# Queries and half of the output gates with the merge gates, scores two chunks ahead, linear attention's heads turn by turn

## The chip, the cores and the metric

One Trainium2 chip, of which the kernel uses one core, with its engines TensorE (PE; its weight loads are PEld), VectorE (DVE), ScalarE (ACT), GpSimd (POOL) and SyncE (SP, which here issues DMAs). The metric is the device time of one execution in microseconds (us), lower is better. All data are float32.

## What is computed

One block of a hybrid model on 1024 frames and 16 meta tokens of width 1024: a feed-forward part, then a mixing part with two branches (attention in a window with sinks, and gated linear attention), then a second feed-forward part. Cut to the mixing part:

```python
u = rmsnorm(h, mix_norm)
(aq, ak, av, gq, gk, gv, gr, g_low, gate_a, gate_b) = split(u @ w_in)
ya = window_sink_attention(aq, ak, av, att_sinks)     # 8 heads of 64, 2 of keys, chunks of 64
log_a = log_sigmoid(g_low @ gla_gate_w + gla_gate_b) / 16
og = gated_linear_attention(gq, gk, gv, log_a)        # 4 heads: 64 of keys, 128 of values
yb = rmsnorm(og, gla_out_norm) * silu(gr)
mixed = sigmoid(gate_a) * (ya @ w_branch_att) + sigmoid(gate_b) * (yb @ w_branch_gla)
h = h + mixed @ w_out
```

The widths are 512 for `aq`, `gv` and `gr` each, 256 for `gq` and `gk`, 128 for `ak` and `av`, and 1024 for each merge gate. Linear attention keeps a state S of each head, S_t = diag(a_t) S_(t-1) + k_t v_t, with output q_t S_t, in chunks: a causal product of scaled queries and keys inside of a chunk, and the state that the chunks before left.

## The kernel before, in words

A float32 matrix is kept as two parts, a high one and the rest (`split`, L101 and L102; weights by `wt.cut`, L125 and L126), and a product of two such matrices is three matmuls: high by high, high by low, low by high (L96 to L98). Columns of `w_in` are taken in blocks of 128, frames in pieces of 512 columns (`CH_FR`) or, with the meta tokens, of 512, 256 and 272 (`CH_T`). So a block over all frames is 2 x 24 matmuls of 512 columns, 96 for two blocks.

Large products go in another way: `Group.product` (L454) makes the four quarters of a product out of seven products of quarters and of their sums. For a pair of blocks these are seven times twelve, 84 matmuls of 512 columns. The sums are made on DVE or POOL (L437), the parts of the weights' quarters on ACT and DVE (L228, L229).

The mixing part in its order:

- **Plain projections** (`together`, L920 on): gk, gq and the first block of gr, as three matmuls each; ACT copies what comes out, and the results go to DRAM (`ev_keep`). As the inputs' parts are made here on ACT and DVE (L808, L812), the first ones run while they come in.
- **Merge gates** (loop at L1104): eight pairs of blocks by seven products. `gate_weights` loads a pair two turns before its use, `gate_out` applies a sigmoid to the first half and writes to `gates` in DRAM. In the last four pairs, `decay` also makes linear attention's scaled queries and keys, and writes them to DRAM.
- **Attention**: keys, values and queries are projected (`firsts`, `q_units`), then 16 chunks are worked off in a loop (L1400). `scores` makes the scores on PE, adds the bias and takes the maxima (L1294) on DVE, the exponentials on ACT (L1299), and scales on DVE (L1300, L1302). `turn` transposes the probabilities and splits them, `attend` multiplies with the values (L1333) and splits the result into `qs`. Scores are made one chunk ahead. To each chunk belongs a slot of `slots`: projections of gv and gr, whose outputs of values are turned later by PE (`ev_tok`, through the list `late`), and then products with `w_branch_att` (`branch_units`, tile `br`), which need attention's result.
- **Linear attention** (class `Gla`, L1446 on): twelve tiles of 512 KB are loaded through SP's queue (L1426). The four heads are two pairs, called heads 0 and 1 in the names; each takes eight steps. A step has the scores of the next step (`products`: tile `at`, L1483, and a masked copy on DVE, L1484), the products with values (`go`, L1490) and with the state (L1493), squares on ACT (L1497) and copies on DVE (L1498), and the update of the state (`kv` on PE, L1502, `st` on DVE, L1504). Head 0 runs all its steps, then head 1; branch products and the output gates (`out_gate`: sigmoid, product, transposes `ot`, and a split) stand between the steps. `end` scales a head's outputs by their norm (L1509 to L1513).
- **Branch products of linear attention** (L1571), then `w_out` and the second feed-forward part.

Outside of `manual_schedule` sections a scheduler orders each engine's instructions by what it assumes of their durations; a tile's next owner waits until the readers of the one before are done. `ttile` gives tiles from pools of four to eight (`g`, `a`, `ga` and more share them), `atile` from a pool of 16, which holds the inputs' parts, then linear attention's tiles.

## Time and profile before

| | us |
|---|---|
| median of 3 runs | 2015.7 |
| lowest and highest | 2015.16, 2017.0 |
| the profiled execution's own time | 2014.66 |
| its span in the trace | 2013.0 |
| PE busy | 1985.8 (99%) |
| DVE busy | 1405.2 (70%) |
| ACT busy | 894.6 (44%) |
| POOL busy | 176.0 (9%) |
| bytes moved by DMA | 343.03 MB, 170 GB/s in the mean |

The span runs from the first to the last instruction; the execution's own time has some us around it. A busy share is the part of the span in which an engine had an instruction in hand. Matmuls overlap in the records: a matmul of 512 columns shows 0.39 us, but the next one starts 0.23 us later, and it is the starts that tell how fast PE goes. The granted clock of PE is 0.997 of full speed in the mean.

### The profile page before, as it was taken

What the parts mean: (1) busy time and instruction counts of PE and PEld (TensorE: products, weight loads), DVE (VectorE), ACT (ScalarE), POOL (GpSimd) and SP (SyncE); (2) the same over time, 40 slices, a digit from 0 to 9 for tenths busy, and PEclk for the clock granted to TensorE, in tenths of its full rate; (3) what the DMA queues carried; (4) which work ended last, traced back from release to release, by engine and by line L of the source; (5) the groups of instructions that cost most, each with busy time, mean ns of one, the idle gap of its engine ahead of it and who ended that gap; (6) DMA issues with size and microseconds to landing.
All of it is one profiled execution on the core that took longest, in us unless ns stands there. A gap on an engine that the chain in (4) does not pass through costs nothing. (4 is left out here: it accounts for less than half of the span.)

```text
span 2013.0 us, 31814 instructions
## 1 busy us (share of the span) xinstructions
PE 1985.8 (99%) x11964; PEld 1757.2 (87%) x11964; DVE 1405.2 (70%) x2449; ACT 894.6 (44%) x1754; POOL 176.0 (9%) x210
## 2 busy tenths in 40 slices
PE   8999999999999999999999999999999999999998
PEld 8999999999999988888888767888888888878887
DVE  6976776675778785466467567568767766757786
ACT  6544444443322254465366445345444544442225
POOL 1000000002323000004100000110000000022220
PEclk9999999999999999999999999999999999999999
DMA  6243443349975333355212646741534543599832
GB/s 215 83 148 127 164 165 127 127 160 375 345 292 196 95 127 108 108 180 174 58 48 69 221 149 213 226 141 53 196 127 134 188 139 126 191 376 353 300 108 84
DMA packets 284618, 343.03 MB, mean 170 GB/s; under 512 B 26406, under 2 KB 192032, under 8 KB 284464
## 3 DMA queue, kind: packets, MB, share of 16 engines
q1 hardware_dynamic: 265376, 274.82, 41.7%
q10 hardware_dynamic: 17296, 61.29, 8.0%
q0 software_dynamic: 1792, 4.89, 0.7%
q8 instruction: 94, 1.54, 0.3%
q14 instruction: 60, 0.49, 0.1%
HBM read 220.66 MB, written 120.27 MB: 169 GB/s over the span
## 5 line engine op out<-in xcount | busy, mean ns | idle before, releaser
L454 PE MATMUL pb<-tt,wop 128*128 128x260 f32 (+1 forms) x2280 | 394.0, 326 | 1.1 <-ACT g L314 1.1
L454 PEld LDWEIGHTS pb<-tt,wop 128*128 128x128 f32 x2280 | 339.0, 188 | 38.3 <-ACT g L314 1.3
L229 DVE TENSOR_TENSOR wop<-s,wop 128x512 fp32r<-128x512 f32 x268 | 190.3, 713 | 116.6 <-ACT wop L228 116.1
L228 ACT CAST wop<-s 128x512 fp32r<-128x512 f32 x268 | 166.0, 621 | 233.9 <-PE pb L454 97.1
L454 PE MATMUL pb<-tm,wop 128*128 128x260 f32 (+1 forms) x1440 | 235.6, 319 | 6.0 <-ACT h L396 4.0
L454 PEld LDWEIGHTS pb<-tm,wop 128*128 128x128 f32 x1440 | 207.8, 189 | 25.9 <-ACT h L396 4.7
L228 ACT CAST wop<-raw 128x512 fp32r<-128x512 f32 x201 | 124.5, 621 | 221.6 <-PE pb L454 106.2
L229 DVE TENSOR_TENSOR wop<-raw,wop 128x512 fp32r<-128x512 f32 x201 | 143.8, 717 | 30.0 <-ACT wop L228 29.9
L454 PE MATMUL pd<-tt,wop 128*128 128x260 f32 (+1 forms) x792 | 138.7, 328 | 0.0
L454 PEld LDWEIGHTS pd<-tt,wop 128*128 128x128 f32 x792 | 118.9, 188 | 13.4
L341 DVE SCALAR_TENSOR_TENSOR h<-pb,h 128x520 f32<-128x520 f32 (+1 forms) x136 | 93.6, 692 | 38.3 <-PE pb L454 36.3
L454 PE MATMUL pd<-tm,wop 128*128 128x260 f32 (+1 forms) x720 | 119.3, 320 | 0.0
L454 PE MATMUL pb<-tb,wop 128*128 128x260 f32 (+1 forms) x696 | 115.7, 319 | 0.7 <-DVE m L742 0.7
L454 PE MATMUL pd<-tb,wop 128*128 128x260 f32 (+1 forms) x696 | 115.5, 319 | 0.0
L454 PE MATMUL pa<-tb,wop 128*128 128x260 f32 (+1 forms) x696 | 115.5, 319 | 0.0
L454 PEld LDWEIGHTS pd<-tm,wop 128*128 128x128 f32 x720 | 104.9, 190 | 9.4
L454 PEld LDWEIGHTS pb<-tb,wop 128*128 128x128 f32 x696 | 100.8, 188 | 10.5 <-ACT vec L87 0.7
L454 PEld LDWEIGHTS pd<-tb,wop 128*128 128x128 f32 x696 | 100.9, 188 | 9.6
L454 PEld LDWEIGHTS pa<-tb,wop 128*128 128x128 f32 x696 | 100.7, 188 | 9.8
L437 DVE TENSOR_TENSOR s<-raw 128x512 f32<-128x512 f32 x92 | 63.3, 688 | 58.6 <-DMA raw<-in_ffn_w_up 53.3
L96 PE MATMUL pj<-uh,whi 128*128 128x512 f32 (+2 forms) x256 | 91.5, 358 | 0.0
L437 POOL TENSOR_TENSOR s<-raw 128x512 f32<-128x512 f32 x28 | 37.7, 1346 | 601.7 <-DMA tm<-f2mid 427.9
(418 smaller groups left out, 3889.2 us busy)
## 6 DMA issues: line engine op xcount, KB each, us to landing
tm<-f1mid ACTq DMA_DIRECT2D x56, 520.0 KB, 6.2
tm<-f2mid ACTq DMA_DIRECT2D x56, 512.0 KB, 5.8
raw<-in_ffn_w_gate SPq DMA_DIRECT2D x42, 512.0 KB, 3.9
raw<-in_ffn_w_up SPq DMA_DIRECT2D x42, 512.0 KB, 4.0
raw<-in_ffn_w_down SPq DMA_DIRECT2D x80, 256.0 KB, 5.7
f2mid<-kh SPq DMA_DIRECT2D x70, 256.0 KB, 2.7
f2mid<-kl SPq DMA_DIRECT2D x70, 256.0 KB, 2.6
f1mid<-kh SPq DMA_DIRECT2D x63, 260.0 KB, 2.7
```

Source lines behind the costliest of these rows:

```text
L96: nc.tensor.matmul(ps, wh[k], xh[k], start=(k == 0), stop=False)
L228: nc.scalar.copy(x[:, 0:n], src)
L229: nc.vector.tensor_sub(x[:, n:2 * n], src, x[:, 0:n].bitcast(F32))
L341: nc.vector.scalar_tensor_tensor(hm, ps, 0.5, hm, op0=ALU.mult, op1=ALU.add)
L437: (eng.tensor_add if add else eng.tensor_sub)(a[s], a[x], a[y])
L454: nc.tensor.matmul(ps, y, z[:, s0:s0 + sn], start=(first and k == 0 and at == 0), stop=(at == 2 and k == len(cols) - 1), skip_group_check= ...
```

## The change

- The two blocks of gq and the blocks 2 and 3 of gr go into the loop of the merge gates as two more pairs, ahead of the eight (`PAIRS`). For gq, `gate_out` scales by 0.125; for gr it makes the sigmoid on ACT and, one product later, the product on DVE, so that `silu(gr)` is stored, and `out_gate` leaves both out for these blocks.
- In the plain projections, gv's blocks 0 and 1 and the first 512 columns of block 2 take the places of gq and of gr's block 0. Their transposes run one call of `together` later.
- Queries 0 and 1 are projected for the first 512 frames ahead of attention, and for the others in its slots. The slots hold those, the rest of gv, gr's blocks 0 and 1, and then the eight branch products that need only the first half of attention's result, as 2, 2, 2, 1 and 1. The weights of the branch and of three other blocks are loaded and cut a second time.
- `scores` runs two chunks ahead, with three tiles `p` in place of two; the reciprocal and the scaling are split off as `finish`.
- The loads of linear attention's tiles are issued on POOL's queue, three in each of the slots 11 to 14.
- The two heads take turns step by step; the masked scores (`attb`), the state and `km` have tiles of each head's own. `end` goes by halves. The output gates of the first half stand at steps 5 to 7 and behind the loop, those of the second half behind the last branch products. The first two branch weights of linear attention are used for the first half of the frames before the second.

```diff
-    plain_views = [cols_view(w_in, c) for c in (C_GK, C_GK + P, C_GQ, C_GQ + P, C_GR)]
+    plain_views = [cols_view(w_in, c) for c in (C_GK, C_GK + P, C_GV, C_GV + P, C_GV + 2 * P)]
...
+    plain_evac = [ev_keep(gk_dram[0]), ev_keep(gk_dram[1]), ev_tok(0), ev_tok(1), ev_tok(2)]
...
+    PAIRS = [("q", 0), ("r", 2)] + [("g", m) for m in range(0, 16, 2)]
...
+    def gate_out(at, i, c, x):
+        what, m = PAIRS[at]
+        cols = slice(c * 512, (c + 1) * 512)
+        if what == "q":
+            nc.scalar.activation(x, x, AF.Copy, scale=0.125)
+            nc.sync.dma_start(out=gq_dram[i, :, cols], in_=x)
+        elif what == "r":
+            g = ttile("g")
+            nc.scalar.activation(g, x, AF.Sigmoid)
+
+            def rest():
+                nc.vector.tensor_mul(x, x, g)
+                nc.sync.dma_start(out=gr_dram[m + i, :, cols], in_=x)
+            late.append(rest)
...
-    for m in range(0, 16, 2):
-        others = [decay(*x) for x in pieces.pop(0)] if m >= KT else []
+    for m in range(len(PAIRS)):
+        others = [decay(*x) for x in pieces.pop(0)] if len(PAIRS) - m <= 4 else []
...
-        s.p = ap_.tile([P, 4, W], F32, tag="p", name="p", bufs=2)
+        s.p = ap_.tile([P, 4, W], F32, tag="p", name="p", bufs=3)
...
+    slots = [[u] for u in (q_late[0], v_late[0], q_late[1], v_late[1], v_late[2], v_late[3], r_late[0], v_late[4], *r_late[1:])]
...
+    slots += [[fill.pop(0) for _ in range(n)] for n in (2, 2, 2, 1, 1)]
...
+        nc.gpsimd.dma_start(out=ins[x, p][:, 0:S], in_=src)
...
     for c in range(16):
-        nxt = None
+        cur = ahead.pop(0)
+        if ahead:
+            ahead[0].finish()
         turn(cur)
-        if c < 15:
-            nxt = scores(c + 1)
+        if c < 14:
+            ahead.append(scores(c + 2))
         if c % 2 == 0 and c < 14:
             values(c // 2 + 1)
+        run_late()
         for u in slots[c]:
             u()
+        for x in (loads[3 * c - 33:3 * c - 30] if c > 10 else []):
+            load_in(*x)
         attend(cur)
-        cur = nxt
...
     heads = [Gla(0), Gla(1)]
-    for _ in range(4):
+    for _ in range(2):
         fill.pop(0)()
-    for p in range(2):
-        g = heads[p]
+    for g in heads:
         g.begin()
         g.products(0)
         g.state()
-        for j in range(8):
-            if j % 2 == 0 and len(fill) > 4:
-                fill.pop(0)()
-            if p == 1 and j in (1, 3, 5, 7):
-                out_gate(j // 4, CH_FR[(j // 2) % 2:(j // 2) % 2 + 1])
+    for j in range(8):
+        if j == 4:
+            for g in heads:
+                g.end(0)
+        if j in (1, 4):
+            fill.pop(0)()
+        if j > 4:
+            out_gate(j - 5, CH_FR[0:1])
+        for g in heads:
             if j < 7:
                 g.products(j + 1)
             g.step(j)
-        g.end()
+    out_gate(3, CH_FR[0:1])
+    for g in heads:
+        g.end(1)
     while fill:
         fill.pop(0)()
-    for c in range(2):
-        for i in (2, 3):
-            out_gate(i, CH_FR[c:c + 1])
+    for i in range(4):
+        out_gate(i, CH_FR[1:2])
```

The change moves instructions at three places. First PE, in linear attention's turns. In the names, `at` are the scores of the next step, `go` with `gv` and `gw` the products with values, `go` with `st` those with the state, `kv` the update; a number at a tile's end is that of the head. Before, the end of head 0's first step and its second:

```order
L1502 MATMUL kv_13144<-gv0_12955,kt0_13072 64x128
L1502 MATMUL kv_13144<-gw0_12959,kt0_13072 64x128
L1483 MATMUL at_13149<-gqm0_12950,gkm0_12948 128x128
L1483 MATMUL at_13152<-gqm0_12950,gkm0_12948 128x128
L1490 MATMUL go_13156<-gw0_12959,attb11_12988 128x128
L1490 MATMUL go_13155<-gv0_12955,attb10_12987 128x128
L1502 MATMUL kv_13167<-gv0_12955,kt0_13072 64x128
L1502 MATMUL kv_13167<-gw0_12959,kt0_13072 64x128
L96 MATMUL br_13174<-qs0_10613,whi_13105 128x512
L97 MATMUL br_13174<-qs1_10614,whi_13105 128x512
L1493 MATMUL go_13155<-st_13147,gqi0_12957 128x128
L1493 MATMUL go_13156<-st_13147,gqi0_12957 128x128
```

After the change, the end of head 0's first turn and head 1's first turn:

```order
L1522 MATMUL go_13259<-st_13218,gqi0_12853 128x128
L1522 MATMUL go_13260<-st_13218,gqi0_12853 128x128
L1531 MATMUL kv_13271<-gv0_12851,kt0_13193 64x128
L1531 MATMUL kv_13271<-gw0_12855,kt0_13193 64x128
L1512 MATMUL at_13276<-gqm1_12963,gkm1_12961 128x128
L1512 MATMUL at_13279<-gqm1_12963,gkm1_12961 128x128
L1519 MATMUL go_13282<-gv1_13033,attb100_13129 128x128
L1519 MATMUL go_13283<-gw1_13037,attb101_13130 128x128
L1522 MATMUL go_13282<-st_13248,gqi1_13035 128x128
L1522 MATMUL go_13283<-st_13248,gqi1_13035 128x128
L1531 MATMUL kv_13294<-gv1_13033,kt1_13223 64x128
L1531 MATMUL kv_13294<-gw1_13037,kt1_13223 64x128
```

Before, the state that `kv_13144` updates is used by the same head's next step, whose own update `kv_13167` and two branch products have been put ahead of the state's products. Now a whole turn of head 1 lies between an update of head 0 and its use, and each turn has scores, values, state and update in the same order.

Second ACT, in the same turns: `sq` are the squares of the outputs, `g` the sigmoid of an output gate. Before, the first gate:

```order
L1497 ACTIVATE sq_13201,ssq_12993<-go_13195 128x128
L1497 ACTIVATE sq_13204,ssq_12993<-go_13196 128x128
L1497 ACTIVATE sq_13224,ssq_12993<-go_13218 128x128
L1497 ACTIVATE sq_13227,ssq_12993<-go_13219 128x128
L1520 ACT_TABLE_LOAD
L1520 ACTIVATE g_13409<-a_13408 128x512
L1497 ACTIVATE sq_13264,ssq_12993<-go_13258 128x128
L1497 ACTIVATE sq_13267,ssq_12993<-go_13259 128x128
```

And after the change:

```order
L1526 ACTIVATE sq_13265,ssq_13141<-go_13259 128x128
L1526 ACTIVATE sq_13268,ssq_13141<-go_13260 128x128
L1553 ACT_TABLE_LOAD
L1553 ACTIVATE g_13536<-a_13534 128x512
L1526 ACTIVATE sq_13288,ssq_13141<-go_13282 128x128
L1526 ACTIVATE sq_13291,ssq_13141<-go_13283 128x128
L1526 ACTIVATE sq_13335,ssq_13141<-go_13329 128x128
L1526 ACTIVATE sq_13338,ssq_13141<-go_13330 128x128
```

The first gate's sigmoid, with the load of its table, has moved from behind the squares of four steps of head 0 to behind those of head 0's first step; head 1's first squares stand behind it.

Third the queues of linear attention's loads. Before, SP's, between other transfers of attention's last chunks:

```order
L893 DMA gr_dram_8735<-g_12651 128x512
L1426 DMA gkm0_12948<-km_dram_9340 128x1024
L1426 DMA gqm0_12950<-qm_dram_9338 128x1024
L1426 DMA gkd0_12952<-kd_dram_9339 128x1024
L1428 DMA gkd0_12952<-km_dram_9336 128x16
L1426 DMA gv0_12955<-gv_dram_8733 128x1024
L893 DMA gr_dram_8735<-g_12742 128x512
L1380 DMA ga_12815<-gates_8730 128x512
L1426 DMA gqi0_12957<-qi_dram_9337 128x1024
L1380 DMA ga_12832<-gates_8730 128x512
L1426 DMA gw0_12959<-gv_dram_8733 128x1024
```

After the change POOL's, where the rows that make attention's biases stand ahead of them (the first row here is the last of these):

```order
L1206 MEMSET bias_10983 64x1
L1420 DMA gkm0_12731<-km_dram_9415 128x1024
L1420 DMA gqm0_12733<-qm_dram_9413 128x1024
L1420 DMA gkd0_12735<-kd_dram_9414 128x1024
L1422 DMA gkd0_12735<-km_dram_9411 128x16
L1420 DMA gv0_12851<-gv_dram_8733 128x1024
L1420 DMA gqi0_12853<-qi_dram_9412 128x1024
L1420 DMA gw0_12855<-gv_dram_8733 128x1024
L1420 DMA gkm1_12961<-km_dram_9415 128x1024
```

The same twelve tiles and two small ones stand in one piece on a queue that has no other transfer near them.

## Rows read from the trace of the kernel before

**Rows 1.** Page, part 1: busy us, share of the span, instructions of each engine.

```profile
PE 1985.8 (99%) x11964; PEld 1757.2 (87%) x11964; DVE 1405.2 (70%) x2449; ACT 894.6 (44%) x1754; POOL 176.0 (9%) x210
```

**Rows 2.** Stages: length; busy PE, PEld, DVE, ACT, POOL; clock, DMA share, GB/s.

```profile
713.00:780.00 67.00, 66.77 (x356) 55.58 (x357) 51.22 (x99) 33.03 (x78) 3.05 (x7) 1.00 0.41 127
800.74:819.87 19.13, 19.13 (x86) 15.77 (x84) 9.33 (x15) 8.56 (x15) 0.00 (x0) 1.00 0.37 110
1010.00:1130.00 120.00, 119.59 (x789) 105.67 (x789) 82.65 (x287) 77.74 (x235) 0.00 (x0) 1.00 0.24 75
1130.00:1146.00 16.00, 14.72 (x75) 12.11 (x74) 9.49 (x27) 7.03 (x21) 1.15 (x7) 1.00 0.86 279
1159.53:1207.93 48.40, 46.14 (x323) 33.07 (x321) 32.07 (x99) 20.89 (x76) 0.00 (x0) 1.00 0.43 140
```

**Rows 3.** PE's waits: awaited tile and line: us in total, times, longest.

```profile
PE br L96 <- ACT qs L1339: 1.2, 1, 1.2
...
PE kv L1502 <- DVE o L1498: 0.3, 1, 0.3
```

**Rows 4.** PE's timeline in a gate pair: start, us, engine, line, operation, count.

```profile
803.46 2.88 PE L454 MATMUL pb<-tt,wop 128*128 128x512 f32 x12
806.18 2.88 PE L454 MATMUL pd<-tt,wop 128*128 128x512 f32 x12
```

**Rows 5.** Attention: waits of DVE and ACT (989 to 1145); DVE's scaling (1010 to 1130).

```profile
DVE sm L1300 <- ACT p L1299: 31.8, 16, 2.2
...
ACT p L1299 <- DVE mx L1297: 24.7, 9, 2.9
...
L1302 DVE TENSOR_SCALAR p<-p,sm 128x210 f32<-128x210 f32 x52 | 13.6, 324 | 0.3
```

**Rows 6.** DMA issues (KB each, median us to landing); tile f2last: issues on POOL, landing.

```profile
gates<-ga SPq DMA_DIRECT2D x16, 256.0 KB, 4.1
...
a<-gr_dram SPq DMA_DIRECT2D x8, 256.0 KB, 2.9
...
f2last<-kl POOLq DMA_DIRECT2D x2, 256.0 KB, 9.7
...
L241 POOL DMA_DIRECT2D f2last<-kl x2: 539/546/552, 1789.6 to 1790.7; - x2
...
DMA to landing us min/median/max: 2.6/4.2/11.6
```

**Rows 7.** The turns: branch matmuls; columns as in rows 2 without ACT and POOL.

```profile
1159.53:1207.93 48.40, 12.36 (x48) 8.62 (x48) 2.76 (x4) 1.00 0.43 140
```

**Rows 8.** PE's timeline of two turns of head 0.

```profile
1177.31 0.49 PE L1483 MATMUL at<-gqm,gkm 64*128 64x128 f32 x4
...
1178.38 0.49 PE L1493 MATMUL go<-st,gqi 64*128 64x128 f32 x4
1178.80 0.32 PE L1502 MATMUL kv<-gv,kt 128*64 128x128 f32 x1
...
1179.17 0.49 PE L1483 MATMUL at<-gqm,gkm 64*128 64x128 f32 x4
...
1181.38 0.50 PE L96 MATMUL br<-qs,whi 128*128 128x512 f32 x1
```

**Rows 9.** The turns: groups of DVE and ACT (busy us, mean ns | idle before).

```profile
L1484 DVE COPY_PREDICATED attb<-tri,at 128x128 f32<-128x128 uint32 x32 | 8.2, 294 | 1.4 <-PE go L1493 0.8 <-PE at L1483 0.6
L1498 DVE COPY o<-go 128x128 f32<-128x128 f32 x30 | 7.8, 285 | 3.9 <-ACT sq L1497 3.8
L1504 DVE SCALAR_TENSOR_TENSOR st<-st,dec,kv 128x128 f32<-128x128 f32 x14 | 4.8, 343 | 2.9 <-PE kv L1502 2.9
...
L1526 DVE SCALAR_TENSOR_TENSOR a<-ot,vec,a 128x512 f32<-128x512 f32 x4 | 3.0, 745 | 0.2 <-PE ot L1525 0.2
...
L1497 ACT ACTIVATE sq<-go 128x128 f32<-128x128 f32 x30 | 8.0, 272 | 23.3 <-PE go L1493 20.2 <-PE at L1483 3.0
L1497 ACT ACTIVATION_READ_ACCUMULATOR sq<-go 128x1 f32 x30 | 5.9, 198 | 0.0
```

More of the change, by code (lines that the diff above doesn't have):

```diff
@@ L971, in hybrid_kernel @@
     low_w = low_weights()
-    together([(2, CH_FR[1]), (3, CH_FR[1])])
+    together([(i, ch) for i in (2, 3) for ch in CH_T[1:]])
     ra.close()
@@ L995, in hybrid_kernel @@
             g8.tops[n][k] = g8.halves(g8.operand(first, "tt"), bs[k])
-    for ch in CH_FR:
-        together([(4, ch)])
+    together([(4, CH_T[0])])
     low_rank(low_w)
+    run_late()
     def halves_of(m, c):
@@ L1232, in hybrid_kernel @@
             u()
+    q_units(1, CH_FR[0:1])[0]()
     held = []
-    for i in range(1, 4):
+    for i in (2, 3):
         units = q_units(i)
         units[0]()
-        if i < 2:
-            units[1]()
-        else:
-            held.append(units[1])
+        held.append(units[1])
     def values(j):
@@ L1360, in __getitem__, with branch_units @@
             return self.v[:, i[1].start // 64:i[1].stop // 64, :]
-    def branch_units(views, y, m0, load, evac, k=4):
+    def branch_units(views, y, m0, load, evac, k=4, chunks=CH_FR):
         state = {}
@@ L1374, in unit @@
             evac(ps, m0 + m, c0, n, l)
-        return [lambda m=m, c=c: unit(m, *c) for c in CH_FR for m in range(2)]
+        return [lambda m=m, c=c: unit(m, *c) for c in chunks for m in range(2)]
     def load_a(m, c0, n):
@@ L1489, in step @@
             for i in range(2):
[L1490 removed]
+                nc.tensor.matmul(pos[i], attb[p][j % 2][i], self.v[i][:, c:c + P], start=True, stop=False, skip_group_check=True)
             for i in range(2):
@@ L1529, in hybrid_kernel @@
     heads = [Gla(0), Gla(1)]
-    for _ in range(4):
+    for _ in range(2):
         fill.pop(0)()
-    for p in range(2):
-        g = heads[p]
+    for g in heads:
         g.begin()
```

118 lines of the change are left out of this document (61 added, 57 removed).

## The prediction

> **What bounds the kernel now.** I read the page's busy shares first: TensorE (PE) is busy 1985.8 of the span's 2013.0 us, 99%, and no other engine reaches 71% [rows 1]. So time goes only where PE gets fewer matmuls, the same ones closer together, or fewer waits. Next the table of stages, for the part of the program that the change touches [rows 2]: PE is busy nearly throughout in the gates and in attention; the turns of linear attention (48.40 us from 1159.53) show it 46.14 us busy, but with overlapping records of some 0.3 us, so busy time says little there. Then the list of what PE waits for [rows 3]: the change's places have eight entries from 1.2 down to 0.3 us, 5.2 us in all. Last PE's timelines, from which I take the spacing from start to start: that is what a matmul costs on a full engine, where its duration is not.
>
> The sum is made against the profiled execution's own 2014.66 us (1.66 us around its span); the median of the three runs, 2015.7, lies 1.04 us above it. A measurement of this kernel can tell about 0.2% from no change, here 4.0 us.
>
> **The change part by part.**
>
> *Queries and half the output gates by seven products.* Two column blocks of queries and two of output gates, 2 x 96 matmuls of 512 columns, become two pairs of 84. Twelve take 2.72 us (803.46 to 806.18) [rows 4], one 0.2267, so 24 fewer are **−5.44 us**. A pair holds PE for 19.13 us and asks 9.33 us of VectorE (DVE) and 8.56 of ScalarE (ACT) [rows 2], so the new scaling, sigmoid and product (1 to 3 us a pair) lie under PE. Blocks of values take the free plain places; their 22 transposes come with them and are missing in attention. New is that the copies of these transposes stand on DVE between the low halves of the inputs, which DVE makes just ahead of their use. DVE is 51.22 of 67.00 us busy in that stage [rows 2], so a copy shows only where both meet: +0.5, bounds 0 and +1.5 (two passes of 0.745 [rows 9]). With that slack PE also finds the gates' first weights ready when it comes there about 5 us earlier: nothing.
>
> *Scores two chunks ahead.* In attention DVE waits 31.8 us for exponentials and ACT 24.7 us for maxima [rows 5]; this looks like the prize. But PE waited for scaled scores once, 0.6 us; its filler hides the rest. So the direct gain is at most 0.6, counted below with the small gaps. What the depth does is pay for thinner filler: a projection of 512 columns is 24 matmuls, 5.44 us, and by such counts 88.5 us of filler become about 71.9. Small gaps of start to start ahead of transposes (1.0 with the 0.6) and the wait for a split output gate (0.6, with 0.1 beside it) mostly go: −1.7. The last chunk's output still holds PE for its 1.2 us [rows 3], because the second half's first branch product needs it. More switches between row tiles and the full array in the first chunks and the plain stage: +1.0, bounds 0 and +1.5. Six slots are thin now: a projection of 256 or 272 columns (2.9 us by half of 5.44) or one branch product (2.72), with a chunk's own 3.7 or so 6.4 to 6.6 us of PE. DVE's own work is 82.65 us in 120 [rows 2], about 13 chunks, less some 15 us of filler's work: 5.2 a chunk, plus 0.4 to 0.7 to evacuate, plus a weight cut in some. Seven weights are cut twice now, some 1.2 us of DVE and 1.0 of ACT each, and their loads double. That is level: +0.7, bounds 0 and +3 (0.5 each).
>
> *Loads from POOL's queue.* Twelve tiles of 512 KB and two small ones leave SP's queue. On POOL only attention's biases stand ahead, long done (POOL is idle from 1010 to 1130 [rows 2]); what holds the loads is their buffers, free after the last projection in the eleventh slot. From there PE has about 41 us of attention, two branch products (5.4) and head 0's opening, some 49 us in all. 6.3 MB want 129 GB/s in that; the stretch that holds most of these loads now moved 279 GB/s [rows 2]. I take 0. POOL's own rows are slower [rows 6]: a rival below. The Trainium skill ("SBUF — State Buffer", "🔬 SBUF: two separate sides") holds that a DMA issued from GpSimd can't get its descriptors written while VectorE runs a two-port mode, and advises another queue. Attention has four candidates a chunk, the scalings of 0.324 us [rows 5], 1.3 us of some 9: if the rule held for them, landings would stretch by a seventh (an estimate), which 49 us still take.
>
> *Heads in turns.* The 48.40 us hold 48 branch matmuls (4 x 2.72 = 10.9), and 25 transposes of outputs and keys (3.0, at 0.12 each) [rows 7]. That leaves 34.5 us for 16 steps of a head, 2.16 each. A step that nothing disturbs stands in [rows 8]: scores 1177.31, then values, state 1178.38, update 1178.80, the next step 1179.17: 1.86 us. The next one has its update cut in two by the state's products, since it waits for the state that the step before made; it ends at 1181.38, 2.21 us. In the new order all 16 turns have the undisturbed sequence, and the other head's turn lies between a state's update and its use: 14 x 1.86 and two last turns without scores and update (1.06) are 28.2 us, **−6.3 us**.
>
> What is late next is DVE or ACT. A turn asks of DVE two masked copies (0.294), two copies (0.285) and the update (0.343), 1.5 us, and of ACT two squares with their sums (0.94), against PE's 1.86 [rows 9]: near, not over. With an output gate, a pair of turns asks up to 4.3 us of DVE against PE's 4.1. And the first gate's sigmoid now stands on ACT right behind head 0's first squares; its input waits for a buffer that is free once a branch result is written (4.1 us), then loads (2.9) [rows 6]. I put its landing some 15 us behind attention's end (1.3 and 0.8 of waits, 5.4 of two products, 0.7 and 7.0), and head 1's first squares are wanted at about 13.4. Together +1.5, bounds 0 and +6.
>
> *Sum:* −5.4 +0.5 −1.7 +1.0 +0.7 −6.3 +1.5 = **−9.7**: 2005.0 in a profiled run, **2006.0** as a median.
>
> **The rivals.**
>
> *The order of turns pays nothing* (0.17): −9.7 + 6.3 = −3.4, 2012.3. For it: counted in the two orders, the switches of tile shape stay (77 and 74), and if each switch has a fixed price, three fewer at about 0.35 (an update cut in two, 2.21 − 1.86) bring 1 us. Against: the 1.86 us were reached with all of a step's switches in them. The Trainium skill ("TensorEngine Tiling (Array Packing)", "Key Properties") says that changing the tiling mode drains TensorE; by that rule this rival is the likely case, and the row of 1.86 us speaks for less.
>
> *ACT holds the turns* (0.09). The first gate's input lands 3 us later still, because SP's queue also carries branch weights and gates, and head 1's squares wait behind its sigmoid: 2009.0. For: ACT takes its instructions in order. Against: PE waits only when the banks of the turns run out.
>
> *Attention is short of cover* (0.09). In the six thin slots DVE sets the pace, +3 us: 2009.0. For: DVE and ACT wait for each other 56 us now. Against: those are the very waits that a second chunk ahead fills.
>
> *Slower: POOL's queue is late* (0.07). Of the trace's large POOL transfers two were issued at 1789.6 and 1790.7, with another just ahead of each, and the slowest took 11.6 us to land [rows 6]: 1.05 MB in about 12 us. So 6.3 MB take 72 us where 49 are there, and PE stands 23 us before the first turns: 2029. It decides where the queue moves less than 129 GB/s. For: no other large POOL transfer in the trace is fast. Against: those are writes in a busy stretch, and the issues themselves take 0.55 us, so twelve are out in 7 us.
>
> *The change doesn't do what it says*: scores two ahead take nothing from PE's time. That is in the forecast but for 0.6 us.
>
> **How the numbers follow.** The forecast has 0.58, with own bounds of 2002 (no new wait, all small gains) and 2011 (upper bounds of the small terms). The range goes on to the first rival: 2001.5 to 2013.0; outside are the slower rival and the edges of the others, 0.2 together. Faster by over 0.2% is under 2011.7: 0.56 of the forecast, the two at 2009 (0.18), a little of the first (0.04), 0.78 in all. Slower is the last rival, 0.07. The rest is within, 0.15.
>
> **What would show it.** Ten pairs in the gates take 191 us (eight take 153), at 19.1 each. In attention PE's list has no entry over 1.5 us. In the turns a head's step is 1.8 to 1.9 us from scores to scores, without waits for squares over 2 us. The twelve loads land within 40 us of the eleventh slot's end and PE waits for none. I'm wrong if steps stay at 2.1 us (the order was not what cost), if PE waits for a load, or if thin slots show PE waiting for DVE.

## The result, and the profile after

The changed kernel's median is 2018.91 us against 2015.13 (22 runs each), a ratio of 1.0014 [1.0007, 1.002], or 2.8 us. (The ratio is the median over pairs of runs; the two medians lie 3.8 us apart.) It is slower, by an amount inside the 0.2% that counts as no change, and 12.9 us above the forecast of 2006.0. The profiled execution took 2018.8 us, its span 2017.0, 4.0 more than before.

The page of the changed kernel, part 1 (answers to [rows 1]) and PE's granted clock in 40 slices:

```profile
PE 1979.2 (98%) x11940; PEld 1755.3 (87%) x11940; DVE 1431.3 (71%) x2486; ACT 905.1 (45%) x1775; POOL 186.4 (9%) x228
...
PEclk9999999999999999999999899999999999999999
```

PE has 24 matmuls fewer and is busy 6.6 us less, yet the span is longer: the saving is there, and PE stands idle for more than that. One slice of the clock is lower, the one with the end of attention. What PE waits for in the changed kernel (answers to [rows 3]):

```profile
PE br L96 <- DVE ga L1403: 6.2, 1, 6.2
PE po L1354 <- DVE ptl L102: 4.8, 6, 1.9
...
PE vt L906 <- ACT v L900: 2.7, 4, 1.0
...
PE br L96 <- ACT qs L1360: 1.2, 1, 1.2
```

The first three lines shown are new, 13.7 us: 13.1 in attention, and 0.6 of the waits for `v` at 775.8, at the end of the plain stage. Where before lost 5.2 us in eight small entries, one branch product now waits 6.2 us for DVE.

The stages of the changed kernel, columns as in [rows 2]: the gates, projections with attention, three stretches inside of these at attention's end, and the turns with the branch products up to `w_out`:

```profile
776.17:968.70 192.53, 192.39 (x850) 158.63 (x849) 115.78 (x196) 107.84 (x185) 3.46 (x12) 1.00 0.41 128
968.70:1166.60 197.90, 184.64 (x1061) 157.99 (x1060) 128.23 (x383) 110.32 (x310) 33.43 (x75) 0.97 0.44 128
1120.00:1130.00 10.00, 10.00 (x64) 8.60 (x63) 6.59 (x21) 7.07 (x23) 2.70 (x5) 1.00 1.03 404
1130.00:1136.00 6.00, 0.28 (x2) 0.01 (x1) 0.30 (x1) 4.03 (x11) 0.00 (x0) 0.69 1.04 351
1136.00:1143.00 7.00, 6.55 (x16) 5.17 (x17) 6.92 (x22) 0.00 (x0) 0.00 (x0) 0.53 0.58 160
1166.60:1270.30 103.70, 102.49 (x597) 80.56 (x596) 79.28 (x175) 48.70 (x126) 1.87 (x11) 1.00 0.58 186
```

From 1130 to 1136 PE and DVE do next to nothing while the DMA engines are full, and in the 7 us behind it the clock is 0.53. The same product of a gate pair comes again 19.04 us later:

```profile
781.72 2.88 PE L454 MATMUL pb<-tt,wop 128*128 128x512 f32 x12
...
800.76 2.88 PE L454 MATMUL pb<-tt,wop 128*128 128x512 f32 x12
```

For the table, both kernels are cut at PE's starts: first plain projection, first gate product, first projection of attention, last output product of attention, first product of `w_out`, PE's last start. These are 713.2, 778.8, 933.7, 1144.3, 1266.3 and 2005.1 in before, and 712.4, 776.2, 968.7, 1166.6, 1270.3 and 2009.1 in the change. The moved matmuls are counted at 0.2267 us for 512 columns [rows 4] and 0.12 for a transpose:

| stage | before | after | measured | moved matmuls | beyond these |
|---|---|---|---|---|---|
| plain projections | 65.6 | 63.7 | −1.9 | −2.5 | +0.6 |
| gates, two pairs more | 154.8 | 192.5 | +37.7 | +38.1 | −0.4 |
| projections and attention | 210.6 | 197.9 | −12.7 | −30.1 | **+17.4** |
| turns and branch products | 122.0 | 103.7 | −18.3 | −10.9 | **−7.4** |
| `w_out` to PE's last start | 738.8 | 738.7 | −0.1 | | −0.1 |

The 2.5 are 22.5 matmuls of 512 columns less (5.1; shorter ones are counted by their columns) and 22 transposes more (2.6), the 38.1 are 168 matmuls. The 30.1 are 169.5 matmuls of 512 columns less (38.4), 48 branch matmuls more (10.9) and 22 transposes less (2.6). Moved matmuls sum to −5.4; so the columns are saved, the turns gain, and attention takes it all back. The stages sum to +4.7; the part ahead of them is 0.8 us shorter, which leaves the span's 4.0 but for rounding.

**How the 6.2 us come about.** Three timelines of the changed kernel at that place (start, us, engine, line, operation, [idle before and what ended it]); first SP's queue, then DVE, then PE:

```profile
1125.16 5.32 SPq L1399 DMA_DIRECT2D ga<-gates  x2
```
```profile
1128.21 0.17 DVE L1314 TENSOR_SCALAR mx<-mx 128x4 f32<-128x4 f32 x1
1135.70 0.69 DVE L1403 TENSOR_TENSOR ga<-br,ga 128x512 f32<-128x512 f32 x1 [7.33 <-DMA ga<-gates]
1136.31 0.17 DVE L1319 RECIPROCAL sm<-sm 128x4 f32<-128x4 f32 x1
```
```profile
1130.00 0.27 PE L1265 MATMUL vt<-ident,vcat 128*82 128x128 f32 x1
1136.45 0.80 PE L96 MATMUL br<-qs,whi 128*128 128x512 f32 x1 [6.17 <-DVE ga L1403]
1137.04 0.63 PE L97 MATMUL br<-qs,whi 128*128 128x512 f32 x1
1137.47 0.63 PE L98 MATMUL br<-qs,wlo 128*128 128x512 f32 x1
...
1142.57 0.40 PE L98 MATMUL br<-qs,wlo 128*128 128x512 f32 x1
1142.80 0.39 PE L96 MATMUL br<-qs,whi 128*128 128x512 f32 x1
```

DVE's next instruction is the product of a branch result with its merge gate (`ga`, L1403). The gate isn't there, so DVE stands 7.33 us with all of the chunk's work behind it, and PE runs dry of it. What keeps the gate: SP's own waits, POOL's 14 issues for linear attention (two of the groups are shown), and the other transfers from 1100 to 1150 (KB each, median us to landing):

```profile
SPq L893 <- ACT g L892: 17.0, 3, 8.8
...
SPq L1399 <- DMA gr_dram<-g: 4.6, 1, 4.6
```
```profile
ga<-gates SPq DMA_DIRECT2D x6, 256.0 KB, 4.3
...
gkm<-km_dram POOLq DMA_DIRECT2D x2, 512.0 KB, 6.5
...
gw<-gv_dram POOLq DMA_DIRECT2D x2, 512.0 KB, 9.7
```

SP's row merges two loads. The first, the one that DVE waits for, is issued at 1125.16; the branch product that it belongs to has begun at 1121.50. It stands in SP's queue behind a write of the last projection's output (`gr_dram`, L893), for which SP waits 8.8 us on ACT, up to 1123. And it is slow: DVE's wait for it ends at 1135.7, 10.5 us after its issue, where the gates' loads took 4.3 us in the median. POOL's 14 loads had been issued together from 1114.2 to 1124.3 and filled the DMA engines; the write of `gr_dram` issued at 1123.07 took 7.0 us too, where the two before it took 2.0 and 2.3. The second load is issued 5.0 us behind the first, since its tile is one of four temporaries that it shares with the output gates, and SP waits 4.6 us for that write to leave it. It lands at 1136.9, before DVE comes to its product at 1137.48, so this wait cost nothing more.

After the stall 14 matmuls start some 0.43 us apart, where 0.23 is usual: 2.8 us more. The 1.9 us wait for `ptl` at 1041.83 is followed by the same: the clock is 0.85 and 0.80 in the two stretches of 5 us from 1040 on, 1.7 us more. So attention's 17.4 us are, within the reading of these rows, 13.1 us of waits and 4.5 of a low clock.

**The turns** in PE's timeline of the changed kernel (answers to [rows 8]):

```profile
1184.75 0.49 PE L1512 MATMUL at<-gqm,gkm 64*128 64x128 f32 x4
...
1186.60 0.49 PE L1512 MATMUL at<-gqm,gkm 64*128 64x128 f32 x4
...
1188.45 0.49 PE L1512 MATMUL at<-gqm,gkm 64*128 64x128 f32 x4
...
1190.31 0.49 PE L1512 MATMUL at<-gqm,gkm 64*128 64x128 f32 x4
```

From scores to scores it is 1.85 to 1.86 us, as forecast, wherever no branch product or output gate stands between two turns.

### The profile page after: what moved, and what is told of

Read it like the earlier page. It is cut to its first block, busy times and chain, and to the rows that moved or that the text cites. A ratio compares the mean times of both kernels' runs of the same rounds, so it can differ in the third digit from the quotient of the medians.

```text
span 2017.0 us, 31885 instructions
## 1 busy us (share of the span) xinstructions
PE 1979.2 (98%) x11940; PEld 1755.3 (87%) x11940; DVE 1431.3 (71%) x2486; ACT 905.1 (45%) x1775; POOL 186.4 (9%) x228
## 5 line engine op out<-in xcount | busy, mean ns | idle before, releaser
L454 PE MATMUL pb<-tt,wop 128*128 128x260 f32 (+1 forms) x2328 | 404.5, 327 | 0.0
L454 PEld LDWEIGHTS pb<-tt,wop 128*128 128x128 f32 x2328 | 348.7, 188 | 37.4
L229 DVE TENSOR_TENSOR wop<-s,wop 128x512 fp32r<-128x512 f32 x276 | 195.3, 710 | 125.6 <-ACT wop L228 116.4
L228 ACT CAST wop<-s 128x512 fp32r<-128x512 f32 x276 | 170.9, 621 | 238.5 <-PE pb L454 92.1
L229 DVE TENSOR_TENSOR wop<-raw,wop 128x512 fp32r<-128x512 f32 x207 | 148.9, 721 | 40.4 <-ACT wop L228 40.2
L454 PE MATMUL pd<-tt,wop 128*128 128x260 f32 (+1 forms) x816 | 143.9, 329 | 0.0
L454 PEld LDWEIGHTS pd<-tt,wop 128*128 128x128 f32 x816 | 123.3, 188 | 14.0
L125 ACT CAST whi<-raw 128x1024 fp32r<-128x1024 f32 x45 | 47.1, 1047 | 63.5 <-DMA raw<-in_w_out 13.9
```

The lines of the kernel that those rows point to most:

```text
L125: nc.scalar.copy(hi[:, 0:cols], raw[:, 0:cols])
L228: nc.scalar.copy(x[:, 0:n], src)
L229: nc.vector.tensor_sub(x[:, n:2 * n], src, x[:, 0:n].bitcast(F32))
L454: nc.tensor.matmul(ps, y, z[:, s0:s0 + sn], start=(first and k == 0 and at == 0), stop=(at == 2 and k == len(cols) - 1), skip_group_check= ...
```

## The experiments

Every ratio is to the kernel before, with its 95% interval; the changed kernel's is 1.0014. The expectations name theories by letters: A, linear attention's loads crowd the DMA engines at attention's end; B, attention's thin slots and DVE's order in them are the loss; D, the branch products' gates come late through SP's queue and their four shared tiles; E, a second chunk ahead is worth little; F, the order of the slots costs; G, the place of the tiles in memory costs (1536 bytes); H, the same for 64 bytes.

### Whose loads hold attention (e1, e2, e3)

e1: the loads back on SP's queue, behind attention's loop.

```diff
-        nc.gpsimd.dma_start(out=ins[x, p][:, 0:S], in_=src)
+        nc.sync.dma_start(out=ins[x, p][:, 0:S], in_=src)
...
-        for x in (loads[3 * c - 33:3 * c - 30] if c > 10 else []):
-            load_in(*x)
...
     att.close()
+    for x in loads:
+        load_in(*x)
```

> The changed kernel, but linear attention's twelve tiles are loaded from SP's queue behind attention's loop, as before the change. Theory A (the burst of loads on POOL's queue makes the gate loads late, DVE stands behind them, PE stands and its clock falls): the 6.2 us wait of PE for the branch's gate product and the stretch at the lower clock behind it are gone, the time falls by 8 to 10 us against the changed kernel, to 2008 to 2011. Theory B (attention's thin slots are the loss): PE's waits for the split probabilities stay and the time falls by 1 us or less, to 2018. Both: the turns keep 1.8 to 1.9 us a step.

e2: the loads stay on POOL, and each is held back by a small copy on POOL that reads the result of the slot's chunk.

```diff
+        nc.gpsimd.tensor_copy(ins[x, p][:, 0:1], qs[1][:, c, 0:1].bitcast(F32))
```

> The changed kernel with its loads still on POOL's queue, but each waits on POOL for a tiny copy out of the attention output of the chunk before, so that three tiles start per slot and not twelve at once. Theory A (the burst): no wait for gate loads over 2 us, the time as with the loads on SP's queue, 2008 to 2011. Rival (POOL's queue itself is slow, its writing of descriptors is held up): the twelve tiles land late, PE waits for them before the first turns, and the time stays at 2017 or rises.

e3: the loads at the change's places, on SP's queue (the first two lines of e1's diff alone).

> The changed kernel with its loads at the same places of the program, but on SP's queue. Theory A: SP is also the queue of the gate loads and takes its transfers in order, so the tiles go out in one piece there as well, ahead of the gates; the gates are as late or later, PE waits 5 us or more, 2017 to 2022. Rival (only POOL's way of issuing does harm): no such wait, 2008 to 2011.

e1 has 1.0004 [0.9995, 1.0013], e2 1.0034 [1.0022, 1.0047], e3 1.0002 [0.9993, 1.0012]. PE's longest wait in attention, first in e1, then in e2, then in e3:

```profile
PE po L1354 <- ACT pth L101: 6.7, 1, 6.7
```
```profile
PE br L96 <- DVE ga L1403: 4.6, 1, 4.6
```
```profile
PE po L1354 <- ACT pth L101: 6.3, 1, 6.3
```

In e1's program the loads stand behind the loop, but the scheduler puts them among the other transfers of attention, in e3 at nearly the same times. The first and the last large one in e1:

```profile
1115.84 0.32 SPq L1420 DMA_DIRECT2D gkm<-km_dram  x1
...
1140.34 0.43 SPq L1420 DMA_DIRECT2D gw<-gv_dram  x1
```

So the loads are spread and not gone (in e1 the DMA engines are 0.96 and 1.02 full in the two stretches of 10 us from 1130 on), and a stall of like length stays, with another name: DVE waits 4.4 us for a gate, ACT 3.6 us for a branch weight (`whi`, L125), and the probabilities' high part waits behind that. Issuing them in one piece from POOL costs some 2 us against this; pacing them (e2) is no better, with 199.7 us for projections and attention and 105.4 for the turns. No run takes the loads out of attention's end, so what they cost there in all is not shown. In none of these does PE wait for a load of linear attention.

### The order on DVE by hand (e4)

e1, with DVE's instructions of attention's loop kept in the order of the program text instead of the scheduler's.

```diff
+    hand = tc.manual_schedule(engines={nc.vector.engine})
+    hand.__enter__()
     for c in range(16):
...
         attend(cur)
+    hand.__exit__(None, None, None)
```

> As the first of these, and DVE keeps the written order in attention's loop, so that the scaling of a chunk's scores stands behind the chunk before's output and not right behind its own maxima, where the trace shows DVE waiting 2.0 to 2.2 us per chunk for the exponentials. Theory B (DVE's order in thin slots costs the rest, some 5 us with the clock's fall behind the first of these waits): DVE's waits for exponentials fall from 24.6 us to under 8, PE's waits for split probabilities from 4.8 to under 1.5 us, the time 3 to 5 us under the first of these, 2004 to 2007. Rival (DVE's work itself is too much for thin slots): waits move elsewhere, the same time as the first within 1.5 us.

1.0368 [1.0353, 1.0382], 2089.15 us. PE's waits in e4:

```profile
PE tp L1338 <- DVE p L1321: 15.2, 8, 4.4
PE po L1354 <- ACT pth L101: 10.6, 5, 4.3
PE po L1354 <- DVE ptl L102: 9.3, 9, 1.9
```

The scheduler puts the reciprocal right behind the maxima, where DVE waits some 2 us a chunk; that looked like the fault (B), but the written order is far worse.

### The gates of the branch products by themselves (e5, e9)

e5: the gates of the eight branch products come in four large tiles of their own, loaded ahead of linear attention's.

```diff
+    def load_early(i):
+        t = atile(f"e{i}")
+        for m in (2 * i, 2 * i + 1):
+            early[m] = t[:, m % 2 * 512:m % 2 * 512 + 512]
+            nc.gpsimd.dma_start(out=early[m], in_=gates[m, :, 0:512])
...
     def load_a(m, c0, n):
+        if c0 == 0:
+            return early[m]
...
+        if c == 11:
+            for i in range(4):
+                load_early(i)
```

> The changed kernel, with the gates of the eight branch products of attention in four tiles of their own that linear attention does not use yet, loaded on POOL's queue ahead of its twelve tiles, in place of the shared temporaries and SP's queue. Theory D (not who loads the twelve tiles matters, as the two runs with the loads on SP's queue gave back only 2 to 3 us and show a stall of 6 to 7 us at another product; the gates, which wait for one of four shared temporaries, come too late and SP's queue stands behind that wait): DVE's waits for gates fall from 12.3 us to under 2, PE's waits of 6 us and the fall of the clock behind them are gone, the time is 8 to 10 us under the changed kernel, 2008 to 2011. Rival (the branch's weights, 256 KB a pair on SP's queue amid 6.3 MB of other loads, are as late): ACT waits for them instead, PE waits 4 us or more, 2014 to 2018.

e9: the same, with e1's loads on SP.

> As e5, with the twelve tiles on SP's queue behind attention's loop, so that only the gates' loads are on POOL's queue. If the burst of loads as such costs anything once the gates have their own tiles, the time falls by over 2 us, to 2007 to 2009; by theory D it is that of e5 within 2 us, 2010 to 2014.

e5 has 0.9978 [0.9968, 0.9987], 2011.68 us: 7.2 us under the change (1.0014 − 0.9978). e9 has 0.9991 [0.9981, 1.0001]. PE's waits in e5:

```profile
PE po L1354 <- DVE ptl L102: 4.0, 4, 1.9
...
PE vt L906 <- ACT v L900: 2.7, 4, 1.0
PE po L1354 <- ACT pth L101: 1.8, 1, 1.8
```

The 6.2 us are gone, and with them the clock's fall behind them; it still falls at 1040 to 1050 (0.66) and 1150 to 1160 (0.83). e9, with linear attention's loads spread over SP's queue from 1116 to 1140, is no better, and has in PE's list:

```profile
PE po L1354 <- ACT pth L101: 4.5, 1, 4.5
```

So the late gates are the larger part (7.2 us) and POOL's issue in one piece the smaller (2 us in e1 and e3). D holds as far as this: e5 takes the gates out of SP's queue, out of the shared tiles and ahead of linear attention's loads at once, and which of the three counts most is not shown. By the timelines above it is the queue and the loads in flight, and not the tile.

### One chunk ahead again (e6)

```diff
     ahead = [scores(0)]
+    ahead[0].finish()
...
-        if c < 14:
-            ahead.append(scores(c + 2))
+        if c < 15:
+            ahead.append(scores(c + 1))
+            ahead[-1].finish()
```

> The changed kernel with scores one chunk ahead and scaled at once, as before the change. Theory E (DVE takes the scaling right behind the maxima in either order, so the second chunk covers little): within 2 us of the changed kernel, 2017 to 2021. Rival (the second chunk is what makes thin slots bearable): PE's waits for transposes and split probabilities rise to 10 us or more, 2024 or more.

1.0071 [1.0057, 1.0085], 2028.72 us, and in e6 PE waits for scaled scores, the wait that before had once, with 0.6 us:

```profile
PE tp L1338 <- DVE p L1321: 19.7, 7, 6.1
```

E falls: the second chunk ahead is worth 11.5 us in the changed kernel (1.0071 − 1.0014 = 0.0057). It pays for the filler that was moved away; whether it buys anything by itself, in the kernel before, was not run.

### The heads in sequence again (e7)

```diff
+    for p in range(2):
+        g = heads[p]
+        g.begin()
+        g.products(0)
+        g.state()
+        for j in range(8):
...
+            g.step(j)
+        for c in range(2):
+            g.end(c)
```

> The changed kernel with linear attention's head 0 ahead of head 1 again, branch products and gates between steps as before the change. By the forecast's term the time rises by 5 to 8 us, to 2024 to 2027, and the steps take 2.1 us in the mean. Rival (the order of turns pays nothing): 2017 to 2021.

1.0039 [1.0026, 1.0053]: the order of turns, with the places of gates and `end` that belong to it, pays 5 us (0.0025; the intervals leave some 3 to 7). The stage takes 107.6 us instead of 103.7.

### The order of the slots (e8), and when the output is taken (e14, e17, e18)

e8: e5, with projections that need no turning between those that do, and the branch products as 1, 2, 2, 2, 1.

```diff
-    slots = [[u] for u in (q_late[0], v_late[0], q_late[1], v_late[1], v_late[2], v_late[3], r_late[0], v_late[4], *r_late[1:])]
+    slots = [[u] for u in (r_late[0], q_late[0], v_late[0], r_late[1], q_late[1], v_late[1], v_late[2], v_late[3], r_late[2], v_late[4], r_late[3])]
-    slots += [[fill.pop(0) for _ in range(n)] for n in (2, 2, 2, 1, 1)]
+    slots += [[fill.pop(0) for _ in range(n)] for n in (1, 2, 2, 2, 1)]
```

> As e5, with the units of attention's slots in another order: output gates first, the queries' second half one slot later and never next to each other, and the eight branch products as 1, 2, 2, 2 and 1, not 2, 2, 2, 1 and 1. Theory F (thin slots that stand next to extra work of DVE are what is left: 2.0 us of wait at 1040 behind the queries' evacuation and 3.4 us at 1150 in the slot with one product, each with the clock's fall behind it): these two stalls go, the time is 4 to 8 us under e5, 2004 to 2008. Rival (the sum of DVE's and ACT's work is the bound, and stalls only move): within 2 us of e5, 2010 to 2014.

0.9974 [0.9964, 0.9983]. The waits for `ptl` and `v` stay, 4.4 and 4.3 us: F isn't borne out; 1 us under e5 is inside both intervals.

e14: e8, and a chunk's product with values (`attend`) is made a slot later, between the next chunk's transposes.

```diff
-        for off, k, vj, vk in kinds:
+        for n, (off, k, vj, vk) in enumerate(kinds):
+            if n == 1 and before:
+                attend(before)
...
-        attend(cur)
+        run_late()
+        last = cur
```

> As e8, with the product of a chunk's probabilities and values put behind the next chunk's first transposes, and the turns of values behind the slot's units and not ahead of them. Theory F (PE comes to the output product before DVE and ACT have split the probabilities, and to the values' turns before ACT has copied them; both wait only because they stand too close): PE's waits for split probabilities (4.4 us) and copies (4.3 us) fall under 2 us together, the time 4 to 7 us under e8, 2003 to 2007. Rival (DVE and ACT are the bound): PE waits elsewhere, within 2 us of e8.

0.9995 [0.9985, 1.0005]. The waits for `ptl` fall to 0.2 us, but this edit also put the turning of values (`run_late`) right behind the projection that it turns, and PE waits there in e14:

```profile
PE vt L906 <- ACT v L900: 9.4, 5, 2.5
```

e17: e14, with `run_late` ahead of the slot's projections, as in the change.

> As e14, with the turns of values ahead of the slot's units again, as in e8. PE's waits for split probabilities stay under 0.5 us and those for copies return to 4 us as in e8, the time 3 to 5 us under e8, 2006 to 2008. Rival (DVE and ACT are the bound): within 2 us of e8, 2009 to 2013.

e18: e14, with values turned behind the next slot's projection.

```diff
+        old = late[:]
+        late.clear()
...
-        run_late()
+        for f in old:
+            f()
```

> As e14, but behind a slot's units stand the turns of the slot before, whose copies ACT made a slot ago. PE's waits for split probabilities and for copies are under 1 us together, the time 6 to 8 us under e8, 2003 to 2005. Rival (DVE and ACT are the bound): within 2 us of e8, 2009 to 2013.

e17 has 0.9967 [0.9956, 0.9978]; its waits for `ptl` are 2.3 us and for `v` 5.7, both over what was expected. e18 has 0.9962 [0.9949, 0.9976], 2008.24 us: it beats both kernels, before by 7.7 us and the change by 10.5 (ratios). That is 2.4 us under e8, not the 6 to 8 that were expected, and the intervals of e5, e8, e17 and e18 overlap. PE's longest waits in e18 are now:

```profile
PE pj L96 <- DVE g L911: 2.0, 1, 2.0
...
PE br L96 <- DVE vz L1279: 1.6, 1, 1.6
```

Its attention takes 187.2 us, where the changed kernel has 197.9 and the count of matmuls gives 180.5. The 6.7 us that remain are about what is left of waits in it (5.5 us) and of the low clock (0.83 in 1060 to 1070 and in 1120 to 1130, 1.7 us each), less the small gaps that before had there.

### The turns alone, and 64 bytes (e10 to e13, e15, e16)

e10: the kernel before with the order of turns alone (the loop of the change's diff over the old slots; scores, states and `km` with tiles of each head's own, `end` by halves, loads on SP).

> The kernel before with only the heads in turns (with the output gates, the halves of the norm and the order of branch products that belong to it). By the forecast's terms, 6.3 us less for the order, 0.7 for the split gate and up to 1.5 of new waits: 2008.5 to 2011. Rival (the order pays nothing): 2014 to 2017.

0.9978 [0.9965, 0.9991]. That is −4.4 us, near the forecast's −4.8 for this part, but not for its reason: `w_out` and what follows had also become faster, where nothing was changed. In before some products take longer than in e10, at the same clock and with no waits; the prediction has no such term. The next three look for what moved.

e11: the kernel before, with the state and `km` in the pool of the turns' tiles, as the change has them.

```diff
-        km = sml.tile([NM, P], F32, tag="km", name="km", bufs=1)
+        km = gp.tile([NM, P], F32, tag="km", name="km", bufs=2)
...
-            self.st = sml.tile([P, P], F32, tag="st", name="st", bufs=2)
+            self.st = gp.tile([P, P], F32, tag="st", name="st", bufs=4)
```

> The kernel before, with the state and the small key tile taken from linear attention's own pool, so that all pools behind the first small one begin 1536 bytes lower; no instruction is added or moved. Theory G (the place of the tiles costs PE 2 to 6% of the spacing in some products): no matmul of the gates over 0.230 us, the table of the second feed-forward part as in e10, the time 3 to 5 us under before, 2010 to 2012. Rival (the slower products in that one profile are chance): the same as before within 1.5 us, 2014 to 2017.

e12: the change, with four unused tiles in the first small pool that put the 1536 bytes back.

```diff
+    for i in range(4):
+        room = sml.tile([P, 96], F32, tag="room", name="room")
+        nc.gpsimd.memset(room[:, 0:1], 0.0)
```

> The changed kernel with 1536 bytes of unused room in the first small pool, so that weights and inputs lie where they lay before the change. Theory G: the slower products are back and the time rises by 3 to 5 us, to 2022 to 2024. Rival: the same as the changed kernel within 1.5 us, 2017 to 2020.

e13 is e10's kernel, profiled once more; its name tells of another.

> A second look at e10 for its profile alone, without rounds: if the fall of the clock behind PE's wait of 0.8 us for the turned keys (1160 to 1167) is there again, it belongs to this kernel and costs it some 3 us; if not, the turns are 3 to 5 us shorter than in e10's profile.

e11 has 1.0003 [0.9991, 1.0015], e12 1.0013 [1.0004, 1.0023]: a shift by 1536 bytes does nothing, G falls. e13's one run took 2008.98 us.

What is left is 64 bytes: the norm factors `rs` of `end` are half as large in the change. e15 takes 64 bytes from the kernel before, e16 gives 64 to the changed one; nothing else differs, and the instructions of e15 stand in the same order on every engine as before.

```diff
-            rs = sml.tile([P, 8, 2], F32, tag="rs", name="rs", bufs=2)
+            rs = sml.tile([P, 8, 2], F32, tag="rs", name="rs", bufs=1)
```

> The kernel before with one buffer for the norm factors in place of two; every engine's instructions stand in the same order, and one of the two sets of operand tiles and the raw weights lie 64 bytes lower. Theory H (this place costs PE 2 to 6% of the spacing in one product of seven): matmuls of 512 columns over 0.229 us are under 30 in 1420 to 1600 where before has 204, the second feed-forward part is 2 to 3 us shorter up to its last stretch, the time 3 to 5 us under before, 2010 to 2012. Rival: the slow products remain, 2014 to 2017.

In e16 it is `bufs=2` to `bufs=4` on `[P, 4, 2]`.

> The changed kernel with four buffers for the norm factors, so that the same tiles lie 64 bytes higher, as before the change modulo 128. Theory H: the slow products come back and the time rises by 3 to 5 us, to 2022 to 2024. Rival: as the changed kernel within 1.5 us, 2017 to 2020.

e15 has 0.9982 [0.9973, 0.9991], e16 1.0035 [1.0023, 1.0046]. PE's timeline in the second feed-forward part, first of before, then of e15:

```profile
1435.54 2.89 PE L454 MATMUL pb<-tt,wop 128*128 128x512 f32 x12
1438.26 2.95 PE L454 MATMUL pb<-tb,wop 128*128 128x512 f32 x12
1441.05 2.96 PE L454 MATMUL pa<-tb,wop 128*128 128x512 f32 x12
1443.85 2.44 PE L454 MATMUL pb<-tt,wop 128*128 128x512 f32 x10
```
```profile
1435.02 2.88 PE L454 MATMUL pb<-tb,wop 128*128 128x512 f32 x12
1437.74 2.88 PE L454 MATMUL pa<-tb,wop 128*128 128x512 f32 x12
1440.46 2.88 PE L454 MATMUL pb<-tt,wop 128*128 128x512 f32 x12
```

Twelve matmuls of a product with `tb` take 2.79 us in before (1438.26 to 1441.05) and 2.72 in e15. The same 200 us then hold fewer of them; rows of before, e15, the change and e16, columns as in [rows 2]:

```profile
1400.00:1600.00 200.00, 200.00 (x877) 164.52 (x876) 146.59 (x232) 93.52 (x163) 0.00 (x0) 1.00 0.47 154
```
```profile
1400.00:1600.00 200.00, 200.00 (x884) 165.66 (x883) 147.82 (x233) 96.18 (x169) 0.00 (x0) 1.00 0.47 157
```
```profile
1400.00:1600.00 200.00, 200.00 (x884) 165.61 (x883) 148.11 (x235) 94.37 (x166) 0.00 (x0) 1.00 0.46 151
```
```profile
1400.00:1600.00 200.00, 200.00 (x877) 164.67 (x876) 147.73 (x233) 93.87 (x164) 0.00 (x0) 1.00 0.45 148
```

So the change holds a gain of 0.21% or 4.2 us (1.0035 − 1.0014) that is none of its three parts: by accident it moves tiles by 64 bytes (H). Without it, the change costs 7 us. And of e10's 4.4 us some 3.6 are this (0.9982); beside it the order of turns is left with about 1 us in the kernel before. e10's profile shows a wait of 0.8 us at the first scores with the clock down to 0.73 behind it, and a turns' stage of 122.5 us; e13's shows neither; with 118.2 us against e15's 120.4, e13 speaks for 2 us. The interval does not settle that.

## Why the prediction was wrong

By its own steps:

- **Columns, −5.44 and +0.5: the columns right, the +0.5 by luck.** The moved matmuls sum to −5.4, and a pair takes 19.04 us. Ten pairs take 192.5 us, forecast 191. The plain stage lost 0.6 beside them, but not to copies of transposes on DVE, as I had it: PE waits 0.6 us there for ACT's copy of a projection.
- **Heads in turns, −6.3 +1.5: right in mechanism and near in size.** A step takes 1.86 us, and e7 puts the order's worth at 5 us in the changed kernel. In the kernel before it is worth 1 or 2 us (e10 and e13 against e15), and of the 7.4 us in the table some 1 to 1.6 are the 64 bytes (the stage differs by 1.1 us between e16 and the change, by 1.6 between before and e15). The rival that the order pays nothing falls for the changed kernel. By the traces' records e7 has 72 switches of tile shape in its turns and the change 71, so a price on each can't make the 5 us; that the state's update comes a turn ahead of its use is what differs in their timelines, where e7 cuts updates in two as before. The Trainium skill ("TensorEngine Tiling (Array Packing)", "Key Properties") says that changing the tiling mode drains TensorE; no run here singles out one switch. ACT did not hold the turns: PE's list has no wait for squares.
- **Thin slots, +0.7 (bounds 0 and +3), and small gaps, −1.7: this is the step that failed.** "That is level" summed DVE's busy time against PE's for a slot, and left out that DVE and ACT stand with all that is queued behind one late operand (7.33 us on DVE), and that the filler's own inputs can be late. Beyond the moved matmuls attention lost 17.4 us: 13.1 us of waits, and 4.5 of the clock's low level behind two of them. e5 shows 7.2 us to be the gates' loads; e17 and e18 take 2 to 3 more by the order of output and turning, inside overlapping intervals. The prediction had the doubled loads in a term of 0.5 us a slot, and not as a gate that stands in SP's queue and then takes 10.5 us to land. (By its own counts the filler that is left is 71.4 us, not 71.9; nothing hangs on it.)
- **Loads from POOL, "I take 0": right as put, wrong in effect.** PE waits for none of them, and the slower rival's 129 GB/s was passed more than twice: the 6.31 MB were issued from 1114.2 on and the last tile, issued at 1124.3, took 11.9 us, so they went at some 285 GB/s, with DVE busy 6.59 us of 10 in the row of 1120 to 1130. The Trainium skill ("SBUF — State Buffer", "🔬 SBUF: two separate sides") holds that VectorE's two-port mode starves a DMA issued from GpSimd. Such a loss does not show here; what hurt was the reverse, that the burst was fast. Amid it a gate's load took 10.5 us instead of some 4, and a write 7.0 instead of 2. I asked when these transfers land, and not what lands later for them.
- **Two chunks ahead, nothing directly: right, but the cover was priced too low.** The rival "attention is short of cover" had +3 us. With one chunk ahead it is 11.5 us (e6), with two the waits of the list.
- **What no step had: 64 bytes, −4.2 us.** The rows held it: seven products of 2.72 are 19.04 us, as in the change, and the pair of [rows 2] takes 19.13, which I took for rounding. In the view of [rows 4] the product behind the two shown takes 2.79.

Sum by measured terms, which overlap a little, since part of the place's gain lies in the turns: −5.4 (columns) +0.6 (plain stage) −5 (turns) −4.2 (place) +17.4 (attention) is +3.4, against 2.8 by the ratio. The stages of the two profiled runs show the place's gain in part only: from `w_out` on they differ by 0.1 us. There the change has 12 matmuls more in the stretch from 1400 to 1780 (2.7 us), but PE's waits for `f2mid` go from 1.2 to 2.4 us, and from 1800 to 1850 its clock is 0.97 where before had 1.00 (1.5 us).

## What to carry to other kernels

Filler that hides a latency has inputs of its own: before it is thinned or changed, follow its last load back through its queue and ask what else is in flight when it goes, since DVE, which worked in order here, passed one late operand on to everything behind it. A look-ahead that seems to save nothing may be what pays for another part of the change, so undo one part at a time before any is dropped. Before a fraction of a per cent is put down to an edit, look at the spacing of instructions that the edit doesn't touch, and shift the tiles without it.

## What the runs showed of the hardware

- **A matmul's spacing depended on 64 bytes of tiles' place.** With 512 columns it is 0.2267 us in most products and 0.230 to 0.241 in some, in before, e11 and e16; in the stretch from 1400 to 1600 the change, e10, e12, e13, e15, e17 and e18 have at most 5 of these in some 880. From 1420 to 1600 before has 204 spacings over 0.229 us, the change none. In the built programs of before, e11 and e16 the tiles of raw inputs, whose pool lies behind the small one, begin at 96 modulo 128 bytes of a partition, and in those of the change, e10, e12 and e15 at 32. Which tile's place it is, and why, was not tried.
- **Idle time of PE was paid twice.** Behind the wait of 6.2 us the granted clock was 0.53 over 7 us, with 14 matmuls 0.43 us apart (the 1.2 GHz level), then 0.23 again (the 2.4 GHz level). Behind the wait of 1.9 us the products `po` start 0.30 us apart instead of 0.12, and in e10 the clock is 0.73 over 7 us behind a wait of 0.8 us. It isn't so behind every wait: in the change PE waits four times from 1158 to 1166, 0.4 to 0.9 us each, and the clock is 1.00 from 1150 to 1167.
- **A burst from POOL's queue filled the DMA engines, and other queues' transfers slowed.** The 6.3 MB went at some 285 GB/s; with the other queues it was 404 and 351 GB/s in the two stretches from 1120 to 1136, at a DMA share of 1.03 and 1.04. Its tiles of 512 KB took 6.5 to 9.7 us to land in the medians, a gate's load of 256 KB on SP's queue 10.5, where 4.3 is the median.
